# Loading and combining w_down's rows in a decoder layer's cross attention, and when the finished halves of the values are added

## The chip, the cores and the metric

The kernel runs on one core of one Trainium2 chip. The metric is the device time of one execution in microseconds (us), the median of several runs. A core has a matrix engine (TensorE, PE in the profile; its weight loads are the row PEld), a vector engine (VectorE, DVE), a scalar engine (ScalarE, ACT), GpSimd (POOL) and SyncE (SP), which asks for DMA transfers. Each engine works through its own queue of instructions in order. It stops at an instruction whose inputs are not there, and all that is queued behind it waits too, whether it needs those inputs or not.

## The reference

One decoder layer on 1024 tokens of width 1024, in float32. Three branches (causal differential attention, trailing-window pooling, cross attention into 256 memory tokens) are gated and merged, and a convolutional feed-forward block of width 2816 follows. Cut to what the change and its surroundings compute:

```python
q_d, k_d, v_d, u_p, q_m, gate_logits = jnp.split(h @ w_in[l], split_pts, axis=-1)

# cross attention, 4 heads of 128, 256 memory tokens
s = jnp.einsum('bshd,bmhd->bhsm', qh, kh) * (DH_MEM ** -0.5)
p = jax.nn.softmax(s, axis=-1)
o = jnp.einsum('bhsm,bmhd->bshd', p, vh)
y_mem = o.reshape(B, S, MEM_WIDTH) @ w_mem_branch[l]

# pooling: window sums over 2, 4, 8, 16 tokens, a product per channel group
outs.append(window_sum / count[None, :, None] - uf[:, :, g])
y = jnp.einsum('bsgc,gcd->bsgd', p, pool_w)
y_pool = (y.reshape(B, S, POOL_WIDTH) * pool_scale) @ w_pool_branch[l]

# feed-forward, far behind
ff = (jax.nn.gelu(g, approximate=True) * v) @ w_down[l]
```

## The kernel before

**Precision.** A float32 operand is split into a high and a low half: ScalarE copies the high one (`wh`, `pth`, `omh`; line 89 or 99), VectorE subtracts to get the low one (`wl`, `ptl`, `oml`; line 90 or 100). `mm3` (lines 102 to 105) then multiplies high by high, high by low and low by high, so each product is three matmuls, and each needs both ScalarE and VectorE ahead of it.

**Combinations.** Some large products are computed by a seven-product scheme (Strassen's) on sums and differences of blocks. For the last product of the layer, the one with `w_down`, the combinations of its rows are made long before they are needed, in the cross attention stage: `down_combinations(k)`, for k from 0 to 10, loads two blocks of 128 rows into a tile `wd` (two DMAs of 512 KB), does four subtractions of 128x512 on VectorE in place, and stores the tile in DRAM (`tw_d[k]`, 1 MB). The tile has two buffers.

**Cross attention** (profile: about 44 to 168 us) runs over four heads j and two halves i of the tokens. `query` projects the queries (`pq`, then `qh`, `ql`). `softmax` computes scores (`pss`), their negated, scaled maximum (`mmx`, lines 711 and 712), the exponentials on ScalarE, the reciprocal of the sums and the scaled weights (`e`, line 720). `turn` transposes the weights on TensorE (`ptx`) and splits them (`pth`, `ptl`); the transposes rotate through two accumulators, so a later one waits until VectorE has read an earlier one. `weigh` multiplies by the memory values (`po`) and splits the result (`omh`, `oml`). `turn` and `weigh` run one step behind `softmax`. Between these stages `weave` puts fillers: `pool_in` (projects the pooling input, `pu`, and stores it in DRAM as `u_d`), the next head's `query`, and two or three `down_combinations`. A scheduler then orders the instructions of each engine from this program.

**Behind it** (168 to 260 us): `branch(0, dt)` multiplies the cross attention's output by column blocks of `w_mem_branch` (`pb`, 24 matmuls each, result `y`, stored as `branch_d`). Between these blocks `pool_group(g)` loads `u` from `u_d`, makes window sums (`sh`, lines 805 to 815), splits them (`ph`, `pl`) and multiplies by `pool_w` (`pwr` from DRAM, split into `pwh`, `pwl`): that product is `py`. The scheduler also draws the first `pb` matmuls up into the end of cross attention.

**The values** (about 405 to 500 us) are again a seven-product scheme. `value_product(name, ws, acc, ...)` makes four pages k (a split of 128x512, `vpage`: `hi` on ScalarE, `lo` on VectorE) and twelve matmuls behind each. `first_out` adds the finished accumulators `vb` to a copy (`vtmp`, line 972, four additions), splits the sums (`vhl`) and stores them. The third product, "T2", gets `first_out` as its `behind`. `tc.issue_after(x)` means that the scheduler places what is issued inside it behind instruction x.

Of the kernel before, what the change touches and what calls it, by code (L numbers as in the profile page):

```python
# [8 lines left out]
F32 = mybir.dt.float32  # L9
# [3 lines left out]
ALU = mybir.AluOpType  # L13
AX = mybir.AxisListType

P = 128
# [4 lines left out]
H = 512  # L21
# [5 lines left out]
CH = CT // 2  # L27
# [14 lines left out]
def kernel(  # L42
# [7 lines left out]
    nc = tc.nc  # L50
# [12 lines left out]
    out = out[0]  # L63
# [13 lines left out]
    def bank(shape=(P, H), name="b1"):  # L77
        return ps1.tile(list(shape), F32, tag="b1", name=name)

    def pbank(shape=(P, H), name="pj"):  # L80
        return ps0.tile(list(shape), F32, tag="pj", name=name)
# [258 lines left out]
    def wsplit(src, shape, raw=None):  # L340

        if isinstance(raw, tuple):
            return raw
        raw = wload(src, shape) if raw is None else raw
        hi = wst.tile(shape, F32R, tag="wh", name="wh")
        lo = wst.tile(shape, F32R, tag="wl", name="wl")
        return hi, lo, split(hi, lo, raw)

    def chunk(w, c0, n=P):
        return w[:, c0:c0 + n].rearrange("(k p) c -> p k c", p=P)  # L350

    def proj_half(o, wh, wl, i):
        for k in range(KT):
            mm3(o, wh[:, k, :], wl[:, k, :], hTh[i][:, k, :], hTl[i][:, k, :], k == 0, k == KT - 1)

    ahead = {}
    with tc.tile_pool(name="kvm", reuse_waits="tile", bufs=1, side="right") as kvp:
# [5 lines left out]
        with tc.tile_pool(name="pa", reuse_waits="tile", bufs=2, side="right") as pa, \  # L363
# [67 lines left out]
            for i in range(2):  # L431
                both = bank2((P, KT, P), "pt2") if i else None
                for g4 in range(2):
                    pt = both[:, 4 * g4:4 * g4 + 4] if i else bank((P, 4, P), "pt")
                    for j in range(4):
                        k = 4 * g4 + j
# [34 lines left out]
            for i in range(2):  # L471
                on("dve", lambda: nc.vector.tensor_scalar(
                    out=rcol[:, i, :], in0=ident, scalar1=0.0, scalar2=rm[i], op0=ALU.mult, op1=ALU.add))
# [188 lines left out]

        mscale = float(P) ** -0.5
        with tc.tile_pool(name="xa", reuse_waits="tile", bufs=2, side="right") as xa:
            def down_combinations(k):

                w = xa.tile([P, 2, 2, H], F32, name="wd", bufs=2)
                for e in range(2):
                    r = (k + e * CH) * P
                    nc.sync.dma_start(out=w[:, e], in_=w_down[r:r + P, :].rearrange("p (h c) -> p h c", h=2))  # L670
                b11, b12, b21, b22 = w[:, 0, 0], w[:, 0, 1], w[:, 1, 0], w[:, 1, 1]
                for o, x0, x1 in ((b12, b12, b11), (b22, b22, b12), (b11, b22, b11), (b21, b21, b22)):
                    nc.vector.tensor_tensor(out=o, in0=x0, in1=x1, op=ALU.subtract)
                nc.sync.dma_start(out=tw_d[k], in_=w)

            qs = {}

            def query(j, i):
                if i == 0:
                    qs[j] = (wsplit(chunk(w_in, C_QM + j * P), [P, KT, P], ahead.pop("q", None))[:2],  # L680
                             xa.tile([P, S], F32R, name="qh"), xa.tile([P, S], F32R, name="ql"))
                (wh, wl), qh, ql = qs[j]
                pq = pbank(name="pq")
                proj_half(pq, wh, wl, i)
                split(qh[:, i * H:(i + 1) * H], ql[:, i * H:(i + 1) * H], pq)

            us = {}

            def pool_in(g, i):
                if i == 0:  # L690
                    us[g] = wsplit(chunk(w_in, C_U + g * P), [P, KT, P], ahead.pop("u", None))[:2]
                wh, wl = us[g]
                pu = pbank(name="pu")
                proj_half(pu, wh, wl, i)
                u = xa.tile([P, H], F32, name="u0")
                nc.scalar.activation(out=u, in_=pu, func=AF.Copy)
                nc.sync.dma_start(out=u_d[g][:, i * H:(i + 1) * H], in_=u)

            es, pts = {}, {}

            def softmax(j, i, t2):
                _, qh, ql = qs[j]
                if t2 == 0:
                    es[j, i] = xa.tile([P, 4, NM], F32, name="e")
                e = es[j, i]
                pss = bank((P, 2, NM), "pss")
                for u in range(2):
                    ts = slice(i * H + (2 * t2 + u) * P, i * H + (2 * t2 + u + 1) * P)
                    mm3(pss[:, u, :], qh[:, ts], ql[:, ts], kmh[:, j, :], kml[:, j, :], True, True)
                mx = small.tile([P, 2], F32, tag="mmx", name="mmx")  # L710
                nc.vector.reduce_max(out=mx, in_=pss, axis=AX.X)
                nc.vector.tensor_scalar(out=mx, in0=mx, scalar1=-mscale, scalar2=None, op0=ALU.mult)
                sm = small.tile([P, 2], F32, tag="msm", name="msm")
                for u in range(2):
                    nc.scalar.activation(
                        out=e[:, 2 * t2 + u, :], in_=pss[:, u, :], func=AF.Exp, scale=mscale,
                        bias=mx[:, u:u + 1], accum_out=sm[:, u:u + 1])
                nc.vector.reciprocal(out=sm, in_=sm)
                for u in range(2):
                    nc.vector.tensor_scalar(  # L720
                        out=e[:, 2 * t2 + u, :], in0=e[:, 2 * t2 + u, :],
                        scalar1=sm[:, u:u + 1], scalar2=None, op0=ALU.mult)

            def turn(j, i):
                e = es.pop((j, i))
                pth = xa.tile([P, 2, H], F32R, name="pth")
                ptl = xa.tile([P, 2, H], F32R, name="ptl")
                for k in range(2):
                    pt = bank((P, 4, P), "ptx")
                    for u in range(4):  # L730
                        nc.tensor.transpose(pt[:, u, :], e[:, u, k * P:(k + 1) * P], ident)
                    split(pth[:, k, :], ptl[:, k, :], pt.rearrange("p a b -> p (a b)"))
                pts[j, i] = pth, ptl

            def weigh(j, i):
                pth, ptl = pts.pop((j, i))
                po = bank(name="po")
                ds = slice(j * P, (j + 1) * P)
                for k in range(2):
                    mm3(po, vmh[:, k, ds], vml[:, k, ds], pth[:, k, :], ptl[:, k, :], k == 0, k == 1)  # L740
                split(omh[j][:, i * H:(i + 1) * H], oml[j][:, i * H:(i + 1) * H], po)

            query(0, 0)
            query(0, 1)
            lag = None
            for j in range(MH):
                stages = []
                for i in range(2):
                    stages.append(lambda i=i: softmax(j, i, 0))
                    if lag:  # L750
                        stages.append(lambda l=lag: turn(*l))
                    stages.append(lambda i=i: softmax(j, i, 1))
                    if lag:
                        stages.append(lambda l=lag: weigh(*l))
                    lag = (j, i)
                fillers = [lambda i=i: pool_in(j, i) for i in range(2)]
                if j + 1 < MH:
                    fillers += [lambda i=i: query(j + 1, i) for i in range(2)]
                for n, k in enumerate(range(max(3 * j - 1, 0), 3 * j + 2)):
                    fillers.insert(2 * n + 1, lambda k=k: down_combinations(k))  # L760
                weave(stages, fillers)
            turn(*lag)
            weigh(*lag)
# [99 lines left out]
    with tc.tile_pool(name="gp", reuse_waits="tile", bufs=2, side="right") as gp_:  # L863
        for dt in range(0, KT, 2):
            mix = None
            for b in (1, 0):
                raws = []
                for e in range(2):
                    w = (grp if e else wst).tile([P, KT, P], F32, tag="raw", name="rawg", bufs=2 - e)
# [42 lines left out]
        def value_product(name, ws, acc, fresh, behind=None):  # L912

            for k in range(4):
                page = wst.tile([P, 2, H], F32R, tag=("wh", "wl")[pages[0] % 2], name="vpage")
                pages[0] += 1
                hi, lo = split2(page[:, 0], page[:, 1], ws[k])
                if k == 0 and behind:
                    with tc.issue_after(hi.ins), tc.issue_after(lo.ins):
                        behind()  # L920
                bh, bl = hop(name, k)
                for t in TS:
                    ts = slice(t * P, (t + 1) * P)
                    mm3(acc[t], bh[:, ts], bl[:, ts], page[:, 0], page[:, 1], fresh and k == 0, k == 3,
                        onto=not fresh)
# [445 lines left out]
    with tc.tile_pool(name="sub", reuse_waits="tile", bufs=4, side="right") as sub:  # L1371
        gs = sub.tile([P, 1], F32, name="gs", bufs=1)
        nc.vector.tensor_scalar(out=gs, in0=cols[:, 1, 44:45], scalar1=1.0 - LAM_INIT, scalar2=None,
                                op0=ALU.mult)
# [378 lines left out]
    for t in (0, 2, 1, 3):  # L1753
        for n, f in enumerate(fs):
            passes(pa, t, f, False, n == len(fs) - 1, False)
        x1 = load_x1(4 + t)
# [5 lines left out]
        with tc.issue_after(scaled.ins):  # L1762
            nc.vector.scalar_tensor_tensor(out=st[:, 5:6], in0=st[:, 3:4], scalar=-0.5 / D, in1=st[:, 2:3],
                                           op0=ALU.mult, op1=ALU.add)
        r = st[:, 6:7]
        rstd_root(r, st[:, 5:6], st[:, 4:5], st[:, 7:8])
        for j in range(2):
            hs = slice(j * H, (j + 1) * H)
            nc.vector.scalar_tensor_tensor(out=c(1, t, j), in0=c(1, t, j), scalar=r, in1=x1[:, hs],
                                           op0=ALU.mult, op1=ALU.add)  # L1770
# [32 lines left out]
```

## Time and profile before

| | |
|---|---|
| Time, median of 3 runs | 1727.67 us (1727.35 to 1729.21) |
| The profiled execution's own time | 1729.14 us |
| Its span, first to last instruction | 1727.3 us |
| Share of the span in which VectorE is busy | 72% |
| Share of the span in which ScalarE is busy | 51% |
| DMA over the whole span | 294.41 MB, 170 GB/s |
| `wd` loads, 22 of 512 KB, median to landing | 5.9 us |
| `wd` subtractions, 44 of 128x512, first and last start | 48.1 and 135.3 us |
| `pwr` asked, `u` (first) asked | 160.4 and 168.4 us |

The engines work at the same time, so the shares do not add up. In the profile's rows "L673" is line 673 of the kernel, `wd<-wd` the tile written and the tile read, and "x4" four instructions in one row. What stands in brackets behind a row is the time that its engine stood idle before it, and the instruction or transfer that ended this. A share over the whole span is an average over stages with different limits, so the stages are looked at one by one.

### The profile page before, as it was taken

Reading aid. Unit: us, or ns where it says so; the run is one execution under the profiler, and the core shown is the slowest. Engines: PE = TensorE matmul, PEld = TensorE weight load, DVE = VectorE, ACT = ScalarE, POOL = GpSimd, SP = SyncE. Lnnn points to the kernel's source line nnn. Section 1 sums busy time; section 2 is a strip of 40 time slices with the busy share of each in tenths; the row PEclk is TensorE's granted clock in tenths of the full one; section 3 lists DMA queues with packets and bytes.
Section 4 is the critical chain, followed back from the end, with each engine's and each line's share of the span. In section 5 each row is a group of like instructions: output and inputs, shape, how many; then the busy total and the mean of one; then the engine's idle time right before and its main releaser. Section 6 shows DMA issues by size and latency. Waiting matters only on the chain.

```text
span 1727.3 us, 22417 instructions
## 1 busy us (share of the span) xinstructions
PE 1711.2 (99%) x8106; PEld 1421.1 (82%) x8106; DVE 1242.6 (72%) x2059; ACT 888.4 (51%) x1585; POOL 45.0 (3%) x103
## 2 busy tenths in 40 slices
PE   9999999999999999999999999999999999999998
PEld 6887888888888888888888888888888888888886
DVE  7765876666666578888866555848888888878466
ACT  5434554444544467777744344645555555543453
POOL 0000000000000011111110000000000000000000
PEclk9999999999999999999999999999999999999999
DMA  8873544444874676665556571573433332583344
GB/s 271 318 275 111 163 152 155 155 149 148 258 232 158 206 229 170 177 181 150 149 193 234 189 214 50 171 226 91 129 112 101 122 93 90 196 303 101 108 145 141
DMA packets 232867, 294.41 MB, mean 170 GB/s; under 512 B 15929, under 2 KB 161590, under 8 KB 230070
## 3 DMA queue, kind: packets, MB, share of 16 engines
q1 hardware_dynamic: 229222, 285.61, 52.0%
q0 software_dynamic: 3520, 7.38, 1.2%
q8 instruction: 64, 1.05, 0.2%
q14 instruction: 45, 0.37, 0.1%
q10 hardware_dynamic: 16, 0.00, 0.0%
HBM read 201.10 MB, written 85.56 MB: 166 GB/s over the span
## 4 chain that ended last, share of the span: by engine, by line
PE 90%; DVE 5%; DMA 2%; ACT 1%; issue 1%; SPq 1%; DVEq 0%; ACTq 0%
PE pa L103 8%; PE pa L105 8%; PE pa L104 8%; PE pb L103 5%; PE pb L104 5%; PE pb L105 5%; PE pss L1166 3%; PE pd L103 2%; PE pd L105 2%; PE pd L104 2%; PE poa L1222 2%; PE pe L105 2%; PE pe L104 2%; PE pe L103 2%; PE pout L105 2%; PE pout L103 2%
## 5 line engine op out<-in xcount | busy, mean ns | idle before, releaser
L89 ACT ACTIVATE wpage<-s 128x512 fp32r<-128x512 f32 x136 | 85.2, 627 | 103.6 <-DVE s L188 38.1
L1570 DVE SCALAR_TENSOR_TENSOR cvt<-gv,cols,cvt 128x1023 f32<-128x1023 f32 x88 | 112.5, 1278 | 15.7 <-ACT cvt L1566 15.6
L90 DVE TENSOR_TENSOR wpage<-s,wpage 128x512 fp32r<-128x512 f32 x136 | 92.8, 688 | 40.1 <-ACT wpage L89 40.0
L1170 DVE CUSTOM_DVE_ANT_0 z<-pss,hbias 128x256 f32<-128x256 f32 (+7 forms) x128 | 94.6, 752 | 25.3 <-PE pss L1166 24.1
L1175 ACT ACTIVATE z<-z,mx 128x256 f32<-128x256 f32 (+7 forms) x128 | 98.9, 773 | 21.2 <-DVE mx L1170 21.0
L103 PE MATMUL pa<-T,wpage 128*128 128x512 f32 x264 | 102.8, 390 | 0.0
L105 PE MATMUL pa<-T,wpage 128*128 128x512 f32 x264 | 102.7, 389 | 0.0
L104 PE MATMUL pa<-T,wpage 128*128 128x512 f32 x264 | 102.7, 389 | 0.0
L1166 PE MATMUL pss<-ks,q 128*128 128x512 f32 (+5 forms) x384 | 86.6, 349 | 1.6 <-DVE mx L1170 1.6
L89 ACT ACTIVATE page<-blk 128x1024 fp32r<-128x1024 f32 (+1 forms) x42 | 41.4, 989 | 85.1 <-PE pe L104 50.6
L90 DVE TENSOR_TENSOR page<-blk,page 128x1024 fp32r<-128x1024 f32 (+1 forms) x42 | 47.5, 1131 | 38.3 <-ACT page L89 38.3
L1166 PEld LDWEIGHTS pss<-ks,q 128*128 128x128 f32 x384 | 62.9, 189 | 11.3 <-DVE mx L1170 6.4
L103 PE MATMUL pd<-page 128*128 128x512 f32 x176 | 68.7, 390 | 0.0
L104 PE MATMUL pd<-page 128*128 128x512 f32 x176 | 68.5, 389 | 0.0
L105 PE MATMUL pd<-page 128*128 128x512 f32 x176 | 68.3, 389 | 0.0
L103 PE MATMUL pa<-hT,wpage 128*128 128x512 f32 x168 | 65.5, 390 | 0.0
L105 PE MATMUL pa<-hT,wpage 128*128 128x512 f32 x168 | 65.4, 389 | 0.0
L104 PE MATMUL pa<-hT,wpage 128*128 128x512 f32 x168 | 65.4, 389 | 0.0
L1222 PEld LDWEIGHTS poa<-aT,v 128*128 128x128 f32 x480 | 60.8, 190 | 3.0 <-ACT srow L1242 1.4
L1222 PE MATMUL poa<-aT,v 128*128 128x256 f32 (+1 forms) x480 | 62.6, 281 | 0.0
L103 PEld LDWEIGHTS pa<-T,wpage 128*128 128x128 f32 x264 | 49.5, 188 | 10.5 <-DVE gv L252 0.3
L104 PEld LDWEIGHTS pa<-T,wpage 128*128 128x128 f32 x264 | 49.6, 188 | 10.4
(429 smaller groups left out, 4969.0 us busy)
## 6 DMA issues: line engine op xcount, KB each, us to landing
q<-q_d SPq DMA_DIRECT2D x64, 256.0 KB, 5.1
wd<-in_w_down_dram SPq DMA_DIRECT2D x22, 512.0 KB, 5.9
tw_d<-wd SPq DMA_DIRECT2D x11, 1024.0 KB
rawv<-in_w_up_dram SPq DMA_DIRECT2D x22, 512.0 KB, 5.6
rawu<-in_w_up_dram SPq DMA_DIRECT2D x22, 512.0 KB, 4.0
ff_d<-cvt SPq DMA_DIRECT2D x22, 512.0 KB, 5.2
blk<-ff_d SPq DMA_DIRECT2D x20, 512.0 KB, 6.3
br<-tw_d SPq DMA_DIRECT2D x20, 512.0 KB, 4.8
```

The source lines that it names most:

```text
L89: copy = nc.scalar.activation(out=hi, in_=src, func=AF.Copy)
L90: nc.vector.tensor_tensor(out=lo, in0=src, in1=hi.bitcast(F32), op=ALU.subtract)
L103: nc.tensor.matmul(o, ah, bh, start=first, stop=False, skip_group_check=onto)
L104: nc.tensor.matmul(o, ah, bl, start=False, stop=False, skip_group_check=onto)
L105: return nc.tensor.matmul(o, al, bh, start=False, stop=last, skip_group_check=onto)
L1166: last["scores"] = nc.tensor.matmul(pss[:, i * H:i * H + m], q[:, j, c, ts], keys, start=(j == 0), stop=(j == 1))
L1170: nc.vector.tensor_tensor_reduce(out=halves(z[:, 0:n]), in0=pss.rearrange("p (a m) -> p a m", a=2)[:, 0:parts, 0:m], in1=halves(biases[h][ ...
L1175: nc.scalar.activation(out=z[:, 0:n], in_=z[:, 0:n], func=AF.Exp, scale=-1.0, bias=mx[:, c:c + 1], accum_out=sm if c else sums[:, h, t:t + 1])
L1222: nc.tensor.matmul(po[:, qs], (vh, vl)[i][:, k, :], w[j][:, ws], start=(n == 0), stop=(n == len(terms) - 1))
L1570: nc.vector.scalar_tensor_tensor(out=cv[:, sh:], in0=u[:, 0:S - sh], scalar=w, in1=cv[:, sh:], op0=ALU.mult, op1=ALU.add)
```

## The change

In cross attention, `down_combinations(k)` is cut in two. The loads become `down_load(k)`: k = 0 is asked between the two halves of the first query projection, and k + 1 at the start of the combinations of k. The four subtractions of each k are placed behind the negated maximum (`mmx`) of the softmax step that was issued last. The store is as before, and the tile keeps its two buffers. In the values, `first_out` of product T2 is placed behind the third page's halves (k = 2) instead of the first's.

```diff
-            def down_combinations(k):
-
-                w = xa.tile([P, 2, 2, H], F32, name="wd", bufs=2)
+            wds = {}
+
+            def down_load(k):
+
+                w = wds[k] = xa.tile([P, 2, 2, H], F32, name="wd", bufs=2)
                 for e in range(2):
                     r = (k + e * CH) * P
                     nc.sync.dma_start(out=w[:, e], in_=w_down[r:r + P, :].rearrange("p (h c) -> p h c", h=2))
+
+            def down_combinations(k):
+
+                if k + 1 < CH:
+                    down_load(k + 1)
+                w = wds.pop(k)
                 b11, b12, b21, b22 = w[:, 0, 0], w[:, 0, 1], w[:, 1, 0], w[:, 1, 1]
-                for o, x0, x1 in ((b12, b12, b11), (b22, b22, b12), (b11, b22, b11), (b21, b21, b22)):
-                    nc.vector.tensor_tensor(out=o, in0=x0, in1=x1, op=ALU.subtract)
+                with tc.issue_after(wds["after"].ins):
+                    for o, x0, x1 in ((b12, b12, b11), (b22, b22, b12), (b11, b22, b11), (b21, b21, b22)):
+                        nc.vector.tensor_tensor(out=o, in0=x0, in1=x1, op=ALU.subtract)
                 nc.sync.dma_start(out=tw_d[k], in_=w)
...
-                nc.vector.tensor_scalar(out=mx, in0=mx, scalar1=-mscale, scalar2=None, op0=ALU.mult)
+                wds["after"] = nc.vector.tensor_scalar(out=mx, in0=mx, scalar1=-mscale, scalar2=None, op0=ALU.mult)
...
             query(0, 0)
+            down_load(0)
             query(0, 1)
...
-                if k == 0 and behind:
+                if k == 2 and behind:
```

The change has few lines, but the scheduler orders the engines' instructions anew. Three places matter. In the changed kernel the subtractions are line 682, the maximum's scaling 721, the reciprocal 727, the scaled weights 729, the store of a combination 683, the load of `u` 810 and that of `pwr` 803.

VectorE at the end of cross attention, from the last scaled maximum to the last low half of the output (`oml`), before:

```order
L712 TENSOR_SCALAR mmx<-mmx 128x2
L718 RECIPROCAL msm<-msm 128x2
L720 TENSOR_SCALAR e<-e,msm 128x256 x2
L90 TENSOR_TENSOR oml_530<-po,omh_526 128x512
L90 TENSOR_TENSOR ptl<-ptx,pth 128x512 x2
L90 TENSOR_TENSOR oml_530<-po,omh_526 128x512
```

The same stretch in the changed kernel:

```order
L721 TENSOR_SCALAR mmx<-mmx 128x2
L682 TENSOR_TENSOR wd<-wd 128x512 x2
L727 RECIPROCAL msm<-msm 128x2
L682 TENSOR_TENSOR wd<-wd 128x512
L729 TENSOR_SCALAR e<-e,msm 128x256 x2
L682 TENSOR_TENSOR wd<-wd 128x512
L90 TENSOR_TENSOR oml_530<-po,omh_526 128x512
L682 TENSOR_TENSOR wd<-wd 128x512
L90 TENSOR_TENSOR ptl<-ptx,pth 128x512
L682 TENSOR_TENSOR wd<-wd 128x512
L90 TENSOR_TENSOR ptl<-ptx,pth 128x512
L682 TENSOR_TENSOR wd<-wd 128x512 x2
```

The eight subtractions of k = 9 and k = 10, which stood much farther up, are now in this stretch, six of them ahead of the last `ptl`.

SyncE at the end of cross attention, from the last store of the pooling input (`u_d`), before:

```order
L697 DMA u_d<-u_1485 128x512
L337 DMA raw<-in_w_mem_branch_dram 128x4x128
L793 DMA pwr<-in_pool_w_dram 128x4x128
L800 DMA u<-u_d 128x1024 x2
L786 DMA branch_d_90<-y 128x1024
```

And in the changed kernel:

```order
L706 DMA u_d<-u_1488 128x512
L337 DMA raw<-in_w_mem_branch_dram 128x4x128
L672 DMA wd<-in_w_down_dram 128x1024 x2
L683 DMA tw_d<-wd 128x2048
L810 DMA u<-u_d 128x1024
L683 DMA tw_d<-wd 128x2048
L810 DMA u<-u_d 128x1024
L337 DMA raw<-in_w_mem_branch_dram 128x4x128
L803 DMA pwr<-in_pool_w_dram 128x4x128
```

The last load of w_down's rows and the last two stores are now here, and `pwr` has moved behind both `u` and one more `raw`. On TensorE the first `py` has moved with it. From the last matmul of the last `po` to the first `py` there were 35 matmuls of `pb`; now the rows read:

```order
L105 MATMUL pb<-omh_523,wl 128x512
L103 MATMUL pb<-omh_524,wh 128x512
L104 MATMUL pb<-oml_528,wh 128x512
L105 MATMUL pb<-omh_524,wl 128x512
L103 MATMUL pb<-omh_525,wh 128x512
L104 MATMUL pb<-oml_529,wh 128x512
L103 MATMUL py<-ph,pwh 128x512 x2
L105 MATMUL pb<-omh_525,wl 128x512
```

Five more `pb` matmuls stand ahead of the first of these rows, behind that `po`: eleven in all ahead of `py`.

VectorE in the values, around `first_out` of product T2, before:

```order
L100 TENSOR_TENSOR vpage<-vw,vpage 128x512
L972 TENSOR_TENSOR vtmp<-ve,vtmp 128x512 x4
L90 TENSOR_TENSOR vhl<-vtmp,vhl 128x512 x3
L100 TENSOR_TENSOR vpage<-vw,vpage 128x512 x3
L90 TENSOR_TENSOR kpage<-rawk,kpage 128x512
```

And in the changed kernel:

```order
L100 TENSOR_TENSOR vpage<-vw,vpage 128x512 x2
L982 TENSOR_TENSOR vtmp<-ve,vtmp 128x512 x2
L100 TENSOR_TENSOR vpage<-vw,vpage 128x512
L982 TENSOR_TENSOR vtmp<-ve,vtmp 128x512 x2
L90 TENSOR_TENSOR vhl<-vtmp,vhl 128x512 x3
L100 TENSOR_TENSOR vpage<-vw,vpage 128x512
L90 TENSOR_TENSOR kpage<-rawk,kpage 128x512
```

Pages 0 and 2 now come first, page 1 between the additions, and page 3 behind the splits.

## The prediction

> **What bounds the kernel now.** I read the first part of the page, then the table of windows by stage, then TensorE's waits in the two stages that the change touches, and last the timeline around each wait.
>
> ```profile
> span 1727.3 us, 22417 instructions
> PE 1711.2 (99%) x8106; PEld 1421.1 (82%) x8106; DVE 1242.6 (72%) x2059; ACT 888.4 (51%) x1585; POOL 45.0 (3%) x103
> ```
>
> TensorE is busy for 1711.2 of 1727.3 us, and the change alters no matmul. A gain can only come out of the 16 us in which TensorE is idle; a loss is whatever makes it wait more. The windows (busy time of PE, PEld, DVE, ACT, POOL, then granted clock, share and rate of the DMA) say how much of the 16 us lies in which stage:
>
> ```profile
> 44.00:120.00 76.00, 74.72 (x373) 62.55 (x372) 55.60 (x112) 29.35 (x68) 0.00 (x0) 1.00 0.82 298
> 170.00:260.00 90.00, 89.95 (x397) 74.04 (x396) 71.67 (x115) 45.92 (x78) 0.00 (x0) 1.00 0.50 164
> 405.00:500.00 95.00, 94.33 (x415) 77.37 (x414) 66.11 (x94) 48.58 (x83) 0.00 (x0) 1.00 0.80 245
> 602.00:1070.00 468.00, 464.07 (x2523) 394.63 (x2522) 337.69 (x762) 283.14 (x617) 40.82 (x76) 1.00 0.60 179
> ```
>
> Cross attention (44 to 168) leaves 1.28 us of idle TensorE before 120; the branch and pool stage behind it (170 to 260) 0.05; the values stage 0.67. So at most about 2 us can be won where the change works. The second row also gives the price of a 128x512 matmul: 90.0 us / 397 = 0.227 us from one start to the next (the longer durations in the timeline overlap).
>
> The table of waits has a single one of TensorE from 44 to 170, for the `ptl` shown in part 1. The chain of work that ended last passes through the DMA just ahead of it:
>
> ```profile
> 101.83 6.26 DMA tw_d<-wd
> 108.11 5.82 DMA wd<-in_w_down_dram
> ```
>
> A load of w_down's rows could be asked only once the store of an older combination had freed its buffer (6.26 us), then took 5.82 us, and VectorE stood still with a subtraction at its head.
>
> **Part 1: the stall that goes.** The timeline of VectorE and TensorE there:
>
> ```profile
> 114.03 0.69 DVE L673 TENSOR_TENSOR wd<-wd 128x512 f32<-128x512 f32 x1 [5.13 <-DMA wd<-in_w_down_dram]
> ...
> 115.90 0.68 DVE L90 TENSOR_TENSOR ptl<-ptx,pth 128x512 fp32r<-128x512 f32 x1
> ```
>
> ```profile
> 114.97 0.39 PE L103 MATMUL pu<-hTh,wh 128*128 128x512 f32 x1
> 116.64 0.66 PE L731 MATMUL ptx<-ident,e 128*128 128x128 f32 x4 [1.28 <-DVE ptl L90]
> ```
>
> VectorE waits 5.13 us, and the `ptl` queued behind the subtraction comes so late that the next transposes start 1.67 us after the matmul before them: 1.67 - 0.227 = **1.44 us** lost. With the load asked a step ahead and the subtraction behind a softmax maximum, that goes: **-1.44**. The buffers remain two, so load k+1 still waits for store k-1; what is late next at this place is another `ptl` that a `wd` now precedes in the queue (one near 72 us). One subtraction is 0.67 us, so 0 to +0.67; I take **+0.2**, because filler matmuls stand ahead of most of these waits.
>
> **Part 2: the values stage.**
>
> ```profile
> 431.23 2.48 DVE L972 TENSOR_TENSOR vtmp<-ve,vtmp 128x512 f32<-128x512 f32 x4
> 433.62 1.96 DVE L90 TENSOR_TENSOR vhl<-vtmp,vhl 128x512 fp32r<-128x512 f32 x3
> 435.50 1.89 DVE L100 TENSOR_TENSOR vpage<-vw,vpage 128x512 fp32r<-128x512 f32 x3
> ```
>
> ```profile
> 435.19 0.61 PE L103 MATMUL vd<-vpage,hT 128*128 128x512 f32 x2
> 436.24 0.50 PE L104 MATMUL vd<-vpage,hT 128*128 128x512 f32 x1 [0.43 <-DVE vpage L100]
> ```
>
> Four additions and three low halves stand between page 0 and page 1 on VectorE, so page 1's low half ends at 436.1. TensorE starts two matmuls from 435.19 and the next at 436.24: 1.05 - 2 x 0.227 = 0.60, and 0.11 more behind that start (0.34 to the next one instead of 0.227): **-0.70**. In the new order page 2 and two additions stand ahead of page 1: two additions (1.2) and three low halves (1.9) less, one page (0.6) more, so VectorE can be done 2.5 us earlier, where 0.7 is needed. What moved behind it is needed later: page 3 at 436.4 or so plus two pages of twelve matmuls, and the next product's writes into `ve` later still. I count nothing for them.
>
> **Part 3: six subtractions in the last softmax.** Before, the last combination is done at 136; now those of k = 9 and k = 10 stand in the tail of cross attention, where the only filler matmuls are `pb`. Six of them come between the last maximum and the last `ptl`.
>
> ```profile
> L673 DVE TENSOR_TENSOR wd<-wd x44: 670/687/696, 48.1 to 135.3; 128x512 f32<-128x512 f32 x44
> ...
> 116.03 0.47 ACT L715 ACTIVATE e<-pss,mmx 128x256 f32<-128x256 f32 x1 [2.23 <-DVE mmx L712]
> ```
>
> Back to back on VectorE one starts 0.60 us after the other (0.687 shown), so six are 3.6 us. Two lie beside the two exponentials (2 x 0.47, 1.0 us with what reads their sums), one beside the copy that makes `pth` (0.6, a ScalarE copy of the shape of `wh` in part 4), and four `pb` matmuls that the new order draws ahead of the last `po` cover 4 x 0.227 = 0.9: 3.6 - 1.0 - 0.6 - 0.9 = **+1.1** (0 if more `pb` matmuls cover the rest, 2.4 if only the exponentials and some 0.2 do).
>
> **Part 4: the first pool product.** This is the large term. Before, 35 `pb` matmuls stand between the last `po` and the first `py`; now eleven do. But what `py` needs starts after that `po`, as SyncE's row shows (`u`'s load waits for it), and `pool_w`'s load, before asked at 160, is now queued on SyncE behind `u`, the last store `tw_d`, the second `u` and `raw`, of which `raw` waits for a `wl`.
>
> ```profile
> 168.01 0.39 PE L105 MATMUL po<-pth,vml 128*128 128x512 f32 x1
> 176.77 0.73 PE L103 MATMUL py<-ph,pwh 128*128 128x512 f32 x2
> ...
> SPq L800 <- PE po L105: 7.5, 1, 7.5
> 168.43 0.81 SPq L800 DMA_DIRECT2D u<-u_d  x2
> ...
> 168.44 0.60 ACT L89 ACTIVATE omh<-po 128x512 fp32r<-128x512 f32 x1 [1.64 <-PE po L105]
> 170.59 0.63 ACT L89 ACTIVATE wh<-raw 128x512 fp32r<-128x512 f32 x1 [1.07 <-PE pb L104]
> 175.65 1.06 ACT L89 ACTIVATE ph<-sh 128x1024 fp32r<-128x1024 f32 x1 [1.93 <-DVE sh L815]
> ...
> 169.07 0.69 DVE L90 TENSOR_TENSOR oml<-po,omh 128x512 fp32r<-128x512 f32 x1 [1.55 <-ACT omh L89]
> 171.26 0.69 DVE L90 TENSOR_TENSOR wl<-raw,wh 128x512 fp32r<-128x512 f32 x1 [1.50 <-ACT wh L89]
> 172.87 0.15 DVE L805 COPY sh<-u 128x1 f32<-128x1 f32 x1
> 175.46 0.16 DVE L815 TENSOR_TENSOR sh<-head,u 128x2 f32<-128x2 f32 x1
> ```
>
> ```profile
> DMA to landing us min/median/max: 3.2/3.2/4.1
> DMA to landing us min/median/max: 2.7/4.0/4.1
> DMA to landing us min/median/max: 3.9/5.9/7.8
> ```
>
> The three landings are those of the tiles `u` (512 KB), `raw` (256 KB, from 100 to 260) and `wd` (512 KB, the busiest time). I count from the start of the last `po`.
>
> Path by `u`: asked at 0.42, landed at 3.6, the sums 172.87 to 175.62 = 2.75 to 6.35, `ph` 1.06 to 7.4; ScalarE then has `pwh` in its queue, of the shape of `wh` (0.63), and `py` needs it: 8.0 at the earliest.
>
> Path by `pool_w`: `oml` ends at 1.75, the `pb` that reads it at 2.2, `wh` 2.8, `wl` 3.5, `raw`'s issue (0.81 / 2 in the row of two) 3.9, then `pwr` is asked. With `raw`'s 4.0 us, as it has the same 256 KB, it lands at 7.9 and `pwh` is ready at 8.55. But 2.5 MB are asked from 0.42 on (`u`, `tw_d`, `u`, `raw`, `pwr`), and at the 298 GB/s of 44 to 120 they take 2.62 million bytes / 298 = 8.8 us: landed at 9.2, ready at 9.85. With `wd`'s median, 10.45. I take 9.0, between the first two.
>
> In that time TensorE has twelve steps of 0.227, 2.72 us. It waits 9.0 - 2.72 = 6.28 in all (some of it perhaps earlier, at a `pb` whose accumulator is freed by a copy behind a `tw_d` store). Before, the same place lost 8.76 - 36 x 0.227 = 0.59. So **+5.7**, from +4.7 (8.0) to +7.15 (10.45). The 24 `pb` matmuls that covered this follow later and win nothing back, since TensorE there is full already.
>
> **Sum.** -1.44 + 0.2 - 0.70 + 1.1 + 5.7 = +4.86. The profiled execution took 1729.14 us (span 1727.3), so it would become 1734.0; carried to the median of 1727.67 that is **1732.5 us**.
>
> [...] For the clock, the trace of before has a row at its start, behind idle time, where small matmuls go at 0.24 us each, while the four transposes of the same 128x128 at 116.64 give way to the next matmul after 0.41 us, 0.10 each:
>
> ```profile
> 1.41 2.40 PE L408 MATMUL idle<-ident 128*128 128x128 f32 x10 [1.41 <-POOL ident masks.py:199]
> ```
>
> Ten at 0.24 instead of 0.10 are 1.4 us lost. If the wait at `py` slowed TensorE likewise, that is the price. [...]
>
> **Rivals.**
>
> *Given back later* (not slower). TensorE idles 3.93 us between 602 and 1070, in the attention blocks. If the other engines use the 6 us wait at `py` to run ahead, and those waits shrink, up to 3.9 comes back: 1732.5 - 3.9 = 1728.6. It decides against "slower" once more than 1.4 us come back. For it: the DMA has more time. Against it: the stages between (170 to 500) leave TensorE 0.05 to 0.7 us idle, so there the others already keep up, and a head start ends at the next buffer. Chance 0.10.
>
> *Low ends*: `pool_w` lands quickly, parts 1 and 3 cost nothing: -1.44 - 0.70 + 4.7 = +2.6, 1730.2. For it: landings of 2.7 occur. 0.20.
>
> *Backlog*: `pwr` lands as `wd` at its median or later, and part 3 costs 2.4: -2.14 + 0.2 + 2.4 + 7.15 = +7.6, 1735.3. For it: one store of 1 MB took 6.26. 0.10.
>
> *The load is still late*, so that the change does not do what it says: load k+1 waits for store k-1 as before, and the 1.44 stays: 1733.9. Against it: the subtractions are now spread over all of cross attention. 0.08.
>
> *The clock falls* in the wait at `py`: +1.4, 1733.9. 0.12.
>
> **How the numbers follow.** Forecast 0.40, the rivals together 0.60. A difference within 0.2% (3.5 us, about what a measurement of this kernel can tell from no change) is "same": slower starts at 1731.1. Forecast, backlog, late load and clock are slower: 0.70. Low ends and given back are same, 0.28 of their 0.30; 0.02 is left for faster (below 1724.2), which would need more than both removed stalls (2.1 us). The range runs from 1727.0 (given back with the lower terms) to 1736.0 (backlog and some of the clock).
>
> **What would show it.** Right: no wait of `ptx` near 115; no wait at `vd` L104 near 435; a wait of 4 to 6 us at `py` L103 behind ACT `pwh`, with `pwr`'s landing as the releaser of `pwh`; TensorE idle by 5 to 7 us around 165 to 180; small waits for `ptl` ahead of the last `po`. Wrong: `py` held for less than 3 us, so that the landing was mis-sized; or a wait at `po` of more than 3 us, which would put the loss in part 3. [...]

## The result and the profile after

| | before | changed |
|---|---|---|
| Time, median | 1728.2 us (6 runs) | 1739.4 us (6 runs, 1737.97 to 1740.8) |
| Ratio to before, 95% interval | | 1.0063, 1.0050 to 1.0076 |
| The profiled execution's own time, span | 1729.14, 1727.3 us | 1737.97, 1736.2 us |

Slower was forecast, by 4.9 us; it became slower by 11 (by 10 in the same comparison made again, e9 below). The windows of the changed kernel show where:

```profile
44.00:120.00 76.00, 76.00 (x380) 63.48 (x379) 46.38 (x98) 29.32 (x68) 0.00 (x0) 1.00 0.58 206
120.00:165.00 45.00, 44.93 (x228) 36.81 (x227) 32.50 (x71) 17.81 (x47) 0.00 (x0) 1.00 0.67 241
165.00:200.00 35.00, 27.97 (x106) 20.28 (x104) 27.89 (x45) 14.38 (x23) 0.00 (x0) 0.90 0.61 207
405.00:502.00 97.00, 96.89 (x426) 79.41 (x425) 65.44 (x93) 47.60 (x82) 0.00 (x0) 1.00 0.75 232
```

The third of these windows in the profile of before:

```profile
165.00:200.00 35.00, 34.95 (x154) 27.93 (x153) 30.54 (x51) 18.02 (x29) 0.00 (x0) 1.00 0.55 181
```

Up to 165 us TensorE is full: the 1.28 us of idle time ahead of 120 are gone. In the values (last row) 0.11 us are left of 0.67. The whole loss is in the 35 us of the third row: 7.0 us idle and a granted clock of 0.90, where before has 0.05 and 1.00. TensorE's waits from 44 to 200 (what waited, for what, us in total, times, longest):

```profile
PE py L103 <- ACT pwh L89: 5.1, 1, 5.1
PE pb L103 <- ACT y L795: 1.0, 1, 1.0
PE pb L103 <- ACT omh L89: 0.7, 1, 0.7
PE pb L104 <- DVE oml L90: 0.2, 1, 0.2
```

And TensorE's timeline, from the last `po` to where the matmuls go at their usual pace again:

```profile
167.34 0.40 PE L105 MATMUL po<-pth,vml 128*128 128x512 f32 x1
168.42 0.49 PE L103 MATMUL pb<-omh,wh 128*128 128x512 f32 x1 [0.69 <-ACT omh L89]
...
170.85 0.50 PE L103 MATMUL pb<-omh,wh 128*128 128x512 f32 x1 [0.97 <-ACT y L795]
...
172.59 0.40 PE L104 MATMUL pb<-oml,wh 128*128 128x512 f32 x1
178.11 1.22 PE L103 MATMUL py<-ph,pwh 128*128 128x512 f32 x2 [5.13 <-ACT pwh L89]
179.13 0.63 PE L105 MATMUL pb<-omh,wl 128*128 128x512 f32 x1
179.56 0.63 PE L103 MATMUL pb<-omh,wh 128*128 128x512 f32 x1
...
182.97 0.50 PE L104 MATMUL pb<-oml,wh 128*128 128x512 f32 x1
183.31 0.40 PE L105 MATMUL pb<-omh,wl 128*128 128x512 f32 x1
```

Two things are to be seen. `py` starts 10.77 us after the last `po`, and in between TensorE has twelve steps of 0.227, 2.72 us: 8.05 us of waiting, where before had 0.59. And behind `py` a matmul starts every 0.43 us (179.13 to 179.56) up to 182.97: eleven starts in 4.86 us instead of 2.50, 2.4 us more lost. Ahead of the wait, SyncE, VectorE and ScalarE show what `py` waited for:

```profile
167.76 0.33 SPq L810 DMA_DIRECT2D u<-u_d  x1
168.25 0.32 SPq L683 DMA_DIRECT2D tw_d<-wd  x1
168.62 0.43 SPq L810 DMA_DIRECT2D u<-u_d  x1
171.06 0.38 SPq L337 DMA_DIRECT2D raw<-in_w_mem_branch_dram  x1
171.49 0.79 SPq L803 DMA_DIRECT2D pwr<-in_pool_w_dram  x1
...
171.98 0.15 DVE L815 COPY sh<-u 128x1 f32<-128x1 f32 x1 [0.95 <-DMA u<-u_d]
175.78 0.15 DVE L815 COPY sh<-u 128x1 f32<-128x1 f32 x1 [1.04 <-DMA u<-u_d]
...
174.77 1.06 ACT L89 ACTIVATE ph<-sh 128x1024 fp32r<-128x1024 f32 x1 [3.49 <-DVE sh L825]
177.43 0.63 ACT L89 ACTIVATE pwh<-pwr 128x512 fp32r<-128x512 f32 x1 [1.60 <-DMA pwr<-in_pool_w_dram]
```

`pool_w` was asked at 171.49, behind 2.25 MB of other transfers, and ScalarE could copy it at 177.43: 5.9 us to land. `ph` had been ready since 175.83.

### The profile page after: what moved, and what is told of

It reads as the page before. It is cut to its first block, busy times and chain, and to the rows that moved or that the text cites. A ratio compares the mean times of both kernels' runs of the same rounds, so it can differ in the third digit from the quotient of the medians.

```text
span 1736.2 us, 22432 instructions
## 1 busy us (share of the span) xinstructions
PE 1714.9 (99%) x8106; PEld 1422.1 (82%) x8106; DVE 1241.3 (71%) x2059; ACT 887.4 (51%) x1585; POOL 45.0 (3%) x103
## 4 chain that ended last, share of the span: by engine, by line
PE 91%; DVE 4%; DMA 3%; SPq 1%; ACT 1%; issue 1%; DVEq 0%; ACTq 0%
PE pa L105 8%; PE pa L103 8%; PE pa L104 8%; PE pb L105 5%; PE pb L104 5%; PE pb L103 5%; PE pss L1176 3%; PE pd L103 2%; PE pd L104 2%; PE pd L105 2%; PE poa L1232 2%; PE pe L105 2%; PE pe L104 2%; PE pe L103 2%; PE pout L105 2%; PE pout L103 2%
## 5 line engine op out<-in xcount | busy, mean ns | idle before, releaser
L89 ACT ACTIVATE wh<-raw 128x1024 fp32r<-128x1024 f32 (+1 forms) x36 | 31.2, 868 | 54.5 <-issue 19.4
L103 PEld LDWEIGHTS pa<-T,wpage 128*128 128x128 f32 x264 | 49.6, 188 | 10.5 <-DVE gv L252 0.3
```

Source lines behind the costliest of these rows:

```text
L89: copy = nc.scalar.activation(out=hi, in_=src, func=AF.Copy)
L103: nc.tensor.matmul(o, ah, bh, start=first, stop=False, skip_group_check=onto)
```

## The experiments

All are compared with the kernel before, in three sets of five rounds each: e1 to e4, e5 to e8, e9 to e12. The full change is 1.0063; its repetition, beside e10 to e12, comes first.

**e9: the full change again.** No edit.

> The full change once more, in the same rounds as the three beside it. Theory: the loss has two parts of its own, a wait of 7.5 us more between the last po and py and matmuls at half pace, and the second part varies with where the idle stretch falls: ratio 1.005 to 1.0075, and the profile shows matmuls at 0.43 us for 5 us or more in all, possibly ahead of py too. Rival (the profiled execution of the full change was a lucky or unlucky one): a wait at py below 3 us, or no half pace.

Measured: 1738.16 us against 1728.44, ratio 1.0058 (1.0046 to 1.0071). `py` waits again, for `pwh`, but only 3.8 us, since this time the matmuls ahead of it already run at half pace (0.43 us from start to start):

```profile
170.91 0.50 PE L103 MATMUL pb<-omh,wh 128*128 128x512 f32 x1 [0.97 <-ACT y L795]
...
171.58 0.63 PE L105 MATMUL pb<-omh,wl 128*128 128x512 f32 x1
172.01 0.63 PE L103 MATMUL pb<-omh,wh 128*128 128x512 f32 x1
...
178.13 1.21 PE L103 MATMUL py<-ph,pwh 128*128 128x512 f32 x2 [3.79 <-ACT pwh L89]
```

What is slow ahead of `py` costs nothing, as `py` is not ready. So the loss ahead of `py` is not the wait in the row of waits. It is the distance from the last `po` (167.40) to `py`: 10.73 us, the same as in the first profile.

**e1 and e2: each half of the change alone.** In e1 only this:

```diff
-                if k == 0 and behind:
+                if k == 2 and behind:
```

> Only the edit in the values stage, cross attention as before. Theory: it removes the wait of TensorE at vd L104 (0.60 + 0.11 us in the profile of before) and adds nothing: -0.7 us, ratio 0.9996 to the kernel before, no row for vd in the waits. Rival (the edit has a share in the 11 us lost): a ratio above 1.001.

Measured: 1.0002 (0.9992 to 1.0011). The wait at `vd` is gone from the profile, but the 0.7 us is less than the interval can show. The profile tells something else. The code of cross attention is that of before here, and yet TensorE has no wait at `ptx` from 44 to 170. VectorE waits for the same load, shorter:

```profile
111.77 0.69 DVE L673 TENSOR_TENSOR wd<-wd 128x512 f32<-128x512 f32 x1 [3.43 <-DMA wd<-in_w_down_dram]
```

3.43 us instead of 5.13. The 1.44 us stall that the prediction took from the profile of before is thus there in one execution and not in another of the same cross attention.

e2 is the change without that edit.

> Only the edits in cross attention, the values as before. Theory: the whole loss is here: ratio about 1.0068 (the full change's 1.0063 plus 0.7 us), the wait at py of 5.1 us and the matmuls at 0.43 us behind it are there again, the wait at vd L104 (0.6 us) too. Rival: less than 1.004, the rest of the loss then being in the values stage or in later stages.

Measured: 1.0062 (1.0050 to 1.0074). The whole loss lies in cross attention's part of the change. `py` waited 3.8 us, with matmuls at half pace ahead of it as in e9 (a start every 0.43 us from 171.67 to 173.81).

**e3: TensorE kept busy.** 24 extra matmuls, whose result nothing reads, are put behind the third `pb` that follows the last `po`. The rest of the edit, not shown, marks that `pb` and the first `py`, and keeps the later `pb` of the second block behind `py`. The line of the extra matmuls is 815 there and `py`'s is 840.

```diff
+            if g == 0:
+                idle = bank2(name="idle2")
+                last = marks["pb", 0, 0]
+                for t in range(24):
+                    with tc.issue_after(last.ins):
+                        last = nc.tensor.matmul(idle[:, 0:H], omh[0][:, 0:P], omh[0][:, 0:H], start=True, stop=True)
```

> The full change, and 24 matmuls of 128x512 whose result nobody reads, on TensorE alone, behind the third pb matmul after the last po, ahead of the other pb and py; the orders of ScalarE, VectorE and SyncE are the full change's. 24 x 0.227 = 5.4 us fill most of the idle 8 us, so no idle stretch is longer than some 1.5 us, and the first py still waits for pwh. Theory (the clock falls because TensorE stands idle): py begins about as late, 10.8 us after the last po, but the matmuls behind it go at 0.227 us, granted clock 1.00, and 2.8 us or more come back: ratio 1.003 to 1.005. Rival (half pace has another cause, a DMA or the place in the program): 0.43 us again and 1.006; without any effect of the wait itself the 24 matmuls would make it slower still, by up to 5 us.

Measured: 1.0051 (1.0039 to 1.0063), 1736.19 us against 1738.7 of e2 in the same rounds: 2.5 us faster with more work, a little less than was named. The timeline:

```profile
168.12 0.40 PE L105 MATMUL po<-pth,vml 128*128 128x512 f32 x1
...
170.51 5.61 PE L815 MATMUL idle<-omh 128*128 128x512 f32 x24
...
178.84 0.50 PE L840 MATMUL py<-ph,pwh 128*128 128x512 f32 x1 [0.68 <-ACT pwh L89]
179.17 0.40 PE L103 MATMUL py<-ph,pwh 128*128 128x512 f32 x1
179.41 0.40 PE L103 MATMUL pb<-omh,wh 128*128 128x512 f32 x1
```

`py` comes 10.72 us after the last `po`, as late as without the extra matmuls, and behind it they go every 0.24 us. The granted clock is 1.00 all through. So the half pace of e2 (0.43 us from start to start) came with TensorE standing idle, and it cost roughly 2 us of the ten (2.5 by these medians, of which the values stage, as before in e2, can be up to 0.7); the other part is the distance itself.

**e4: `pool_w` asked early.**

```diff
+        pwr = opool.tile([P, 4, P], F32, name="pwr")
...
                 weave(stages, fillers)
+                if j == 2:
+                    nc.sync.dma_start(out=pwr, in_=pool_w.rearrange("g c d -> c g d"))
...
-        pwr = plp.tile([P, 4, P], F32, name="pwr", bufs=1)
-        nc.sync.dma_start(out=pwr, in_=pool_w.rearrange("g c d -> c g d"))
```

> The full change, and pool_w's load into a buffer of its own asked in front of the last head instead of behind raw on SyncE. py stays where it is on TensorE (ten pb ahead instead of eleven). Theory (pool_w's landing at 177.4 is what py waits for last, and the u path, ph ready at 175.8, is next): py starts about 8.5 us after the last po instead of 10.8, and with a wait of about 3.2 us in one piece the clock may or may not fall: 2.3 to 5 us less than the full change, ratio 1.0035 to 1.005. Rival (u's landing behind the stores of tw_d is the bound, pool_w only comes with it): less than 0.5 us changes.

Measured: 1.0050 (1.0038 to 1.0062). `py` is held by the next input now:

```profile
167.60 0.40 PE L105 MATMUL po<-pth,vml 128*128 128x512 f32 x1
...
176.38 0.73 PE L103 MATMUL py<-ph,pwh 128*128 128x512 f32 x2 [1.53 <-ACT ph L89]
```

8.78 us instead of 10.77: `pool_w`'s landing was worth 2.0 us, and without it the path by `u` still keeps `py` waiting. Matmuls went at half pace here too, on both sides of `py` (a start every 0.43 us from 172.10 to 174.23 and from 179.00 to 181.98).

**e5 and e6: the tie and the load ahead, one at a time.** e5 asks the loads a step ahead and leaves the subtractions untied; e6 ties them and asks each load with its own combination.

```diff
 e5
-                with tc.issue_after(wds["after"].ins):
+                if True:
 e6
-                if k + 1 < CH:
-                    down_load(k + 1)
+                down_load(k)
...
-            down_load(0)
```

> The full change without placing the subtractions behind the maximum; the loads are still asked a step ahead. In this order the last combination is done well ahead of the last scores, pool_w's load stands ahead of u's on SyncE, and 36 steps lie between the last po and the first py, as before the change. Theory (the tie, by moving two combinations into the tail, costs everything): no wait at py, no half pace, ratio 0.9985 to 1.0003. Rival (loads asked a step ahead crowd the DMA): above 1.003.

Measured: 0.9996 (0.9987 to 1.0005), no wait at `py` and a clock of 1.00.

> The full change with the loads asked at the start of their own combination, as before; the tie stays. The order at the end of cross attention is the full change's (eleven pb ahead of py, pool_w behind raw). Theory (the tie alone costs): ratio about 1.006, a wait of 4 to 5 us at py and matmuls at 0.43 us. Rival (the load ahead is needed for the loss): below 1.002.

Measured: 1.0048 (1.0035 to 1.0060). The loss is there without the load ahead, so the tie is enough for it. Its place in the timeline is not the one that was expected:

```profile
167.83 0.40 PE L105 MATMUL po<-pth,vml 128*128 128x512 f32 x1
...
175.33 1.09 ACT L793 ACTIVATE y<-pb 128x512 f32<-128x512 f32 x2 [4.52 <-DVE sh L823]
175.98 0.80 PE L103 MATMUL pb<-omh,wh 128*128 128x512 f32 x1 [5.61 <-ACT y L793]
...
179.13 0.46 PE L104 MATMUL pb<-oml,wh 128*128 128x512 f32 x1
179.42 0.62 PE L103 MATMUL py<-ph,pwh 128*128 128x512 f32 x2
```

TensorE waits 5.6 us at a `pb` for the copies `y`, which start at 175.33, and `py` then does not wait at all. The row puts the wait of `y` down to `sh`, which `y` does not read. The trace's semaphore records name another: ahead of that copy ScalarE's queue waits for the semaphore of the last store `tw_d`, asked at 168.75, and its last update comes at 174.94. In the full change the copy does not wait for that store. The likely reason, not shown, is that `y` has the place of that `wd` in memory here. It is the case that the prediction had put in brackets, a `pb` whose accumulator is freed by a copy behind a `tw_d` store. The distance is 11.6 us.

**e8: `py` later.** The second block of `pb` comes ahead of the first pool group, and the first `py` behind its last matmul.

```diff
-                mm3(pb, bh[:, k, :], bl[:, k, :], yh[k][:, hs], yl[k][:, hs], k == 0, k == 3)
+                marks["pb", b, dt] = mm3(pb, bh[:, k, :], bl[:, k, :], yh[k][:, hs], yl[k][:, hs], k == 0, k == 3)
...
-                mm3(py, pwh[:, g, :], pwl[:, g, :], ph[:, hs], pl[:, hs], True, True)
+                with tc.issue_after(marks["pb", 0, 1].ins) if g == 0 else nullcontext():
+                    mm3(py, pwh[:, g, :], pwl[:, g, :], ph[:, hs], pl[:, hs], True, True)
...
         branch(0, 0)
+        branch(0, 1)
         for g in range(4):
             pool_group(g)
-            branch(0, g + 1)
-        for dt in range(5, KT):
+            branch(0, g + 2)
+        for dt in range(6, KT):
             branch(0, dt)
```

> The full change with the first py placed behind the whole second block of pb (27 of them instead of eleven). What py needs is ready as late as in the full change, 10.8 us after the last po; TensorE has 27 x 0.227 = 6.1 us of work and about 2.5 us of waits for omh, oml and y in that time, so some 2 us of wait at py are left. Theory (the loss is py's place against late inputs, and the clock behind it): ratio 1.001 to 1.003, at the upper end if the waits ahead already slow the clock. Rival (the wait is held by something that moves along with py): 1.006.

Measured: 1.0034 (1.0021 to 1.0046), a little above the range that was named. The first `py` no longer waits (178.32, against 178.01 for the matmul before it), so the inputs were late only against where `py` stood. What is left is the waits for `omh`, `oml` and `y`, half pace behind them from 171.10 to 174.26 (0.43 us and more from start to start), and 1.55 us at the fourth group's `py` (203.59), where the edit has moved the blocks of `pb` as well.

**e7, e12: fewer combinations in the last head.** The eleven combinations are shared out over the heads as 4, 4, 3, 0 (e7) or 3, 3, 3, 2 (e12) instead of 2, 3, 3, 3. All else is the full change.

```diff
-                for n, k in enumerate(range(max(3 * j - 1, 0), 3 * j + 2)):
+                for n, k in enumerate(((0, 1, 2, 3), (4, 5, 6, 7), (8, 9, 10), ())[j]):
```

> The full change with the eleven combinations shared out as 4, 4, 3, 0 over the four heads instead of 2, 3, 3, 3: tied and asked ahead, but none in the last head. 39 steps stand between the last po and the first py, pool_w is asked ahead of u. Theory: as the full change without its tail: ratio 0.9985 to 1.0003. Rival (the tie costs wherever it is, by holding up VectorE in each softmax, or four combinations in a head crowd the DMA): above 1.002, with waits of TensorE for ptl or e in heads one to three.

Measured: **0.9986 (0.9977 to 0.9995)**, 1726.49 us against 1728.51. Faster than both kernels. In its windows TensorE is full all through, at a clock of 1.00:

```profile
44.00:120.00 76.00, 76.00 (x381) 63.44 (x380) 53.32 (x109) 29.37 (x68) 0.00 (x0) 1.00 0.73 264
120.00:165.00 45.00, 45.00 (x230) 37.17 (x229) 30.54 (x66) 19.18 (x50) 0.00 (x0) 1.00 0.58 195
165.00:200.00 35.00, 35.00 (x154) 28.04 (x153) 32.77 (x53) 17.31 (x28) 0.00 (x0) 1.00 0.54 185
```

`pool_w` is asked ahead of `u` again there, and 39 steps lie between the last `po` (163.06) and `py` (171.91), without a wait: 39 x 0.227 = 8.85 us, just the distance. So the tie costs nothing where it moves no combination into the last head.

> The full change with the combinations shared out as 3, 3, 3, 2: one combination in place of two in the last softmax, 30 steps between the last po and py instead of twelve, pool_w asked right behind u, ahead of raw. Inputs of py ready about 8.5 us after the last po (u path as in the full change, ph at 8.5), TensorE has 6.8 us of work and a wait for omh and oml of up to 1.4. Theory: 0 to 1.5 us of wait are left at py, ratio 0.999 to 1.0015. Rival (each combination in the last head costs alike): 1.004, two thirds of the full change.

Measured: 0.9997 (0.9988 to 1.0005). One combination in the last softmax costs next to nothing where two cost ten us, because another order comes with it: `pool_w` is asked at 167.03, right behind both `u`, and `py` follows 8.69 us after the last `po` (165.73 to 174.42), over 31 steps. The wait for `y` (0.97) is the only one left in the row of waits.

**e10, e11: which part of e7 is faster than before.** e10 is the kernel before with only the new sharing out; e11 is e7 with the values stage as before.

> The kernel before with nothing changed but the sharing out of its combinations, 4, 4, 3, 0 over the heads: no tie, no load ahead, values as before. Theory (what made e7 faster than the kernel before is that the subtractions no longer stand at the head of VectorE's queue waiting for their load, so the tie or the load ahead are needed): 0.9995 to 1.001, VectorE waiting for wd's load 7 us or more as before. Rival (it is the sharing out alone): 0.9975 to 0.9992, as e7.

Measured: 0.9995 (0.9986 to 1.0005). VectorE waited 4.0 us in all for `wd`'s loads, not 7.

> e7 (4, 4, 3, 0, tied, asked ahead) with the values stage as before. Theory (the values edit is worth the 0.7 us of its wait): 0.0004 slower than e7, 0.9990 or so, and the wait at vd L104 in the profile. Rival (e7's gain is all in cross attention): as e7, 0.9986.

Measured: 0.9990 (0.9982 to 0.9999). The wait at `vd` (0.5 us) is back. The three intervals of e7, e10 and e11 overlap. That e7 is faster than the kernel before is shown; how its 2 us divide among sharing, tie, load ahead and values is not.

## Why the prediction was wrong, point by point

**What bounds the kernel**: right. All of the loss is idle or slowed TensorE, and the matmuls are the same.

**Part 1, the stall at `ptx`**: it went, but it should not have been counted in full. It is in one profile of this code (1.44 us) and not in the other (e1), so a median need not hold all of it. The 0.2 us for another delayed `ptl` did not come: TensorE is not idle at all from 44 to 120.

**Part 2, the values**: the wait went, as worked out (0.67 us of idle time became 0.11). In the time it is too small to be shown.

**Part 3, the six subtractions**: mis-sized, 1.1 us forecast. They stood where the order said, and TensorE lost 0.33 us. From the first `pb` to the last `po` it takes 46 steps in 10.10 us (157.24 to 167.34), before 42 steps in 8.86 (159.15 to 168.01); of the 1.24 us more, 4 x 0.227 = 0.91 are the four `pb` more. What the subtractions do is not in their own time: with the tie they push two combinations, their loads and their stores of 1 MB into the last head, and the scheduler's order of everything behind changes with them (e5, e7, e12).

**Part 4, the first pool product**: the mechanism and the place were right, the size too small. The path by `pool_w` was forecast to be ready 9.0 us after the last `po`, and was after 10.77. It was asked at 4.15 us (3.9 in the sum), but took 5.9 us to land where the sum had about 4.5, between `raw`'s 4.0 and the 5.3 of 298 GB/s. The loads could be read in the order in which they were asked (the first `u` at 171.98, the second at 175.78, `pool_w` at 177.43), and from the first `u` asked (167.76) that makes 2.62 million bytes in 9.7 us, 271 GB/s. So `raw`'s row was the wrong price. The row of `wd` in the busy stretch (5.9), the prediction's far end, has the right number, in part by luck, since those loads are twice as large. That is 7.46 us instead of 5.7. On the path by `u`, `ph` was ready at 8.5, not 7.4, with `u` landing after 4.2 us instead of 3.2.

**The clock**: given as a rival at 0.12 with +1.4 us, and left out of the sum. That was the step that failed most. The prediction itself had a wait of 6.28 us at one place in its sum, and gave that wait no effect on what followed it. Behind `py` the half pace cost 2.4 us in the first profile, 1.7 in e9 (eight starts in 3.53 us from 178.13) and 2.8 in e2 (13 starts in 5.71 us from 178.26). The windows of the changed kernel show the clock fall and return:

```profile
174.00:176.00 2.00, 0.00 (x0) 0.00 (x0) 0.96 (x4) 1.06 (x1) 0.00 (x0) 1.00 1.05 370
176.00:178.00 2.00, 0.00 (x0) 0.00 (x0) 2.00 (x2) 0.57 (x1) 0.00 (x0) 0.59 1.11 389
178.00:180.00 2.00, 1.89 (x5) 1.50 (x6) 2.00 (x4) 0.06 (x1) 0.00 (x0) 0.50 1.05 374
182.00:184.00 2.00, 2.00 (x7) 1.54 (x7) 1.78 (x4) 1.37 (x3) 0.00 (x0) 0.70 0.00 0
```

The last matmul ahead of the wait ends at 173.0. A mean of 0.59 from 176 to 178, between 1.00 and 0.50, puts the fall at 176.4: 3.4 us of idling. The return comes at 183.2 by the same reckoning, 5.1 us after `py` and 6.8 after the fall. TensorE was still idle in the first 1.7 of these 6.8. Both times are one execution's: in e6, behind a wait of 5.61 us, the matmuls start 0.43 us apart from 176.57 to 179.13, and in e9 the first of them do so behind waits of 0.97 us at most. The last section has what these executions showed.

**Given back later**: this did not happen. TensorE stands idle for 3.74 us in the attention blocks (604 to 1078), where it was 3.93, and the lag behind the kernel before is 8.3 us at the end of the values (601.87 and 610.18) and at the layer's last products (1719.65 and 1727.96). **The sum**: 7.46 for `py`, 2.4 for the clock, 0.33 for part 3, less 1.44 and about 0.6 of the removed waits, is 8.1, against 8.83 between the two profiled executions. The same matmuls in both profiles say where the rest is: from the first `pb` to the last of the 192 that read `omh` and `oml` it takes 54.75 us before (159.15 to 213.90) and 65.70 after (157.24 to 222.94). Of these 10.95 us the three terms make 10.2, and small steps of 0.30 to 0.34 us at the later `py` the rest. The medians are 10 to 11 apart. The execution of before that was profiled held the 1.44 us stall, and the changed kernel's was the fastest of its six, so the two profiles may understate the difference. Between the forecast of 4.9 and the measured 10 to 11, then, the clock makes 2.4 and `pool_w`'s landing 1.8; that the medians hold the removed stall only in part is argued, not shown.

## What to carry to other kernels

Tying off-path work behind a late instruction can cost little by its own time (0.33 us here); what to price is everything that the order moves with it, above all loads that a product waits for and the number of matmuls left ahead of that product. Count the steps from the last matmul that releases a load to the first that needs it, and compare them with the whole path, each landing at the price of a stretch equally full of transfers. Where such a sum holds a wait of several us for TensorE in one place, price what may follow it as well: behind the waits of 5.13, 3.79 and 3.77 us at `py` (first profile, e9, e2), matmuls at half pace cost 1.7 to 2.8 us.

## What the runs showed of the hardware that was not expected

In e9 the clock fell without any long idle stretch. TensorE's longest wait ahead of the slow matmuls was 0.97 us; three waits (0.69, 0.23 and 0.97 us by the rows' brackets, 1.9 us in all) within the 3.1 us from 167.8 to 170.9 were followed by starts 0.43 us apart. In the first profile of the same kernel the same three waits were followed by starts 0.23 us apart (171.19 to 172.59). In e3, where the first two came and extra matmuls took the third's place, the starts were 0.23 us apart as well (175.96 to 177.77). So it is not the length of one wait that tells these cases apart.

The traces' clock records have the stretches at 0.50: in e9 from 171.36 to 174.77 and from 178.18 to 181.59, in the first profile from 176.35 to 183.18, in e2 from 170.50 to 173.91 and from 177.33 to 184.16. Two windows of e9, one of the first profile and three of e2, ahead of the falls and in the slow stretches, read:

```profile
167.94:171.36 3.42, 1.67 (x5) 0.89 (x6) 1.65 (x3) 2.10 (x4) 0.00 (x0) 1.00 0.73 210
171.36:174.77 3.41, 2.98 (x8) 1.78 (x6) 2.65 (x5) 0.02 (x1) 0.00 (x0) 0.50 0.98 372
...
172.94:176.35 3.41, 0.04 (x1) 0.00 (x0) 2.27 (x6) 1.06 (x1) 0.00 (x0) 1.00 1.02 356
...
167.09:170.50 3.41, 2.09 (x6) 0.78 (x5) 1.98 (x4) 1.18 (x3) 0.00 (x0) 1.00 0.48 143
170.50:173.91 3.41, 2.83 (x7) 2.25 (x8) 2.40 (x5) 1.02 (x3) 0.00 (x0) 0.50 0.96 357
177.33:180.74 3.41, 2.48 (x6) 2.00 (x7) 2.81 (x4) 0.63 (x1) 0.00 (x0) 0.50 1.07 373
```

Ahead of its first fall TensorE was busy for 1.67 of 3.42 us in e9 (0.49), for 2.09 of 3.41 in e2 (0.61) and for 0.04 of 3.41 in the first profile (0.01). In the slow stretches it was busy for 2.98 of 3.41 us ahead of e9's first return (0.87), for 2.83 ahead of e2's (0.83), and for 2.48 (0.73) in the first half of e2's second, longer one. What sets the clock is not shown by these windows. The bounds are rough: the ends of matmuls are modelled, and six profiles with half pace are all there is.

The slowed stretch ahead of the wait in e9 cost nothing (`py` 10.73 us after the last `po`, against 10.77 in the first profile, where none lay ahead); the one behind the wait in the first profile cost about half its length (2.4 of 4.86 us).
